# Decoder block in fp32 on one core: bias rows of the attention from ScalarE's queue, and other places for the sums of down's weights

## The chip, the cores and the metric

The kernel runs on one core of one Trainium2 chip. The metric is the device time of one execution in microseconds, the median of several; lower is better. The engines are named as in the profile: PE is TensorE, DVE is VectorE, ACT is ScalarE, POOL is GpSimd, SP is SyncE. Every engine works through its own program in order, and they wait for one another by semaphores.

## The reference

One residual block on 512 tokens of width 1024, one layer, everything in float32:

```python
h = rms_norm(x, norm1_g[l]) * (1 + scale1) + shift1
z = h @ w_in[l]
q, k, v, p, g_attn, g_pool = jnp.split(z, split_at, axis=-1)
...
attn = moba_attention(q, k, heads(v), rel_bias)
...
merged = (jax.nn.sigmoid(g_attn) * (attn @ w_branch_attn[l])
          + jax.nn.sigmoid(g_pool) * (pool @ w_branch_pool[l]))
x = x + gate1 * (merged @ w_out[l])
h2 = rms_norm(x, norm2_g[l]) * (1 + scale2) + shift2
u = causal_dwconv(h2 @ w_up[l], conv_w[l], conv_b[l])
u_g, u_v = jnp.split(u, 2, axis=-1)
x = x + gate2 * ((jax.nn.silu(u_g) * u_v) @ w_down[l])
```

The attention has 8 heads of 64 channels and a T5 bias on the logits that depends on the head and on the distance of query and key; with 512 tokens it is plain causal attention. shift, scale and gate (six groups of 1024) are `silu(c) @ ada_w + ada_b`. `w_up` is 1024 x 5632, `w_down` 2816 x 1024.

## The kernel before

Each fp32 matmul is done as three: both operands are split into a high part (`hi`, rounded to the matmul's type by ACT, L113) and a low part (`lo`, the remainder, subtracted by DVE, L123 or L219, in up also L1042), and hi·hi, lo·hi and hi·lo are summed (L132 to L134). So each block of weights needs a load by SP, ACT for hi and DVE for lo before PE can use all of it. The programs of PE, DVE and ACT stand in the order in which the code issues them; POOL and SP mostly issue DMAs, also in order. Buffers come from a pool of 72 tiles of 128x512 (`slot`), five raw weight tiles and 8 PSUM banks.

The stages follow one another: projections of p, q, k and v; the attention, a loop over heads h = 0 to 7; the branch loop, j = 0 to 7, in which the two branches are multiplied by their weights (`br`) and merged; the out stage over four token tiles t; the up stage, j = 0 to 21, each j a pair of a gate block and a value block, from j = 4 on every second one in a form with fewer matmuls; and down, in which products of sums of blocks are used.

**Bias rows.** `fd` in DRAM holds one row of bias per head. `logits(h)` first fetches that row shifted by one element for each partition into a slot, `trev` (L576, a DMA issued by POOL), then PE computes S (L587), DVE adds the bias and takes the minimum (L596), and ACT takes the exponential (L600); `softmax` scales by the reciprocal of the sum (L609 DVE, L610 ACT). In the loop over heads, `logits(h + 1)` and `softmax(h + 1)` are issued at the head of iteration h, after `flip(h)`, which transposes the probabilities of head h (PT). Behind them stand matmuls of the gates, the transposes and norms of Q and K for later heads (`stacks`), the product with v (`values(h)`, L637, which needs PT_l from DVE, L219), and two columns of the adaLN product (`ada_col`, L206 on DVE).

**Sums of down's weights.** Down needs sums of four blocks of `w_down`. They are formed once ahead, in eleven channel tiles kk = 0 to 10. `t_get(kk)` issues four loads of 256 KB on SP (L748); `t_do(kk)` forms four sums on DVE (L753 to L756, in place) and writes them to DRAM (`tsum`) with four DMAs issued by POOL (L758), from where down loads them. In the loop over heads iteration h issues `t_get(h)` for h < 5 and `t_do(h - 1)` for h = 1 to 5. The branch loop holds t_get 5 and 6 (j = 0, 1) and t_do 5 and 6 (j = 1, 2); the out stage t_get 7, 8, 9 and t_do 7, 8, 9 after `out_norm(t)`; up has t_get(10) ahead of j = 0 and t_do(10) at the end of j = 1. In the out stage POOL also issues the loads of x for the residual (L883, for t = 2 and 3 while the stage runs) and stores of the new x (`x2d`, L902); DVE adds to x (L892), forms the norm (xn, L899) and the low parts of the transposed h2 (`h2l`, L875).

**adaLN columns.** `ada_col(5, k)`, k = 0 to 7, runs in up at the j that `ADA_AT[k]` names.

Of the kernel before, what the change touches and what calls it, by code (L numbers as in the profile page):

```python
# [15 lines left out]
P = 128  # L16
S = 512
D = 1024
H = 8
# [36 lines left out]
def block_kernel(tc, x, cvec, ada, wtok, wch, pool_w, wbr, wout, wup, wdn, pack, table, out):  # L56
    nc = tc.nc
# [3 lines left out]
    with ctx:  # L61
# [11 lines left out]
        def slot(name, dt=F32, w=512):  # L73
            return sp.tile([P, w], dt, tag="s", name=name)
# [148 lines left out]
        fd = dpool.tile([H, NF], F32, name="fd")  # L223
# [278 lines left out]
        def fill(gen, us):  # L502
            while us > 0:
                c = next(gen, None)
                if c is None:
                    return
                us -= c
# [61 lines left out]
        ath, atl = [], []  # L569
        apair = {}  # L570

        def logits(h):

            trev = slot(f"trev_{h}")
            fsrc = fd[h : h + 1, :]
            nc.gpsimd.dma_start(  # L576
                trev, bass.AP(tensor=fsrc.tensor, offset=fsrc.offset, ap=[[1, P], [1, 512]]))
            ta = trev[:, :]
            pss = []
            for qt in (3, 2, 1, 0):  # L580
                n = max((qt + 1) * P, 256)
                if qt:
                    sb = bank(f"S_{h}_{qt}")
                    sps = sb
                else:
                    sps = sb[:, 256:]
                nc.tensor.matmul(sps[:, :n], Q[h][:, tslice(qt)], K2[h][:, :n], start=True, stop=False)  # L587
                nc.tensor.matmul(sps[:, :n], Q[h][:, tslice(qt)], K1[h][:, :n], start=False, stop=True)
                pss.append(sps)
            rows, sms = [], []  # L590
            for i, qt in enumerate((3, 2, 1, 0)):
                n = (qt + 1) * P
                L = slot(f"L_{h}_{qt}")
                mn = mini.tile([P, 1], F32, tag="mn", name=f"mn_{h}_{qt}")
                rev = bass.AP(tensor=ta.tensor, offset=ta.offset + n - 1, ap=[list(ta.ap[0]), [-1, n]])
                nc.vector.tensor_tensor_reduce(  # L596
                    out=L[:, :n], in0=pss[i][:, :n], in1=rev, op0=ALU.add, op1=ALU.min, scale=1.0,
                    scalar=3e38, accum_out=mn)
                sm = mini.tile([P, 1], F32, tag="sm", name=f"sm_{h}_{qt}")
                nc.scalar.activation(L[:, :n], L[:, :n], AF.Exp, scale=-1.0, bias=mn, accum_out=sm)  # L600
                rows.append(L)
                sms.append(sm)
            return rows, sms

        def softmax(h, rows, sms):
# [115 lines left out]
        fill(vgen, 1)  # L721
        stacks(0, True)
        fill(vgen, 2)
        stacks(1, True)
        stacks(0, False)
        fill(vgen, 5.5)
# [35 lines left out]
        def t_get(kk):  # L762
            tb[kk] = t_load(kk)

        def t_do(kk):
            t_forms(kk, tb.pop(kk))
# [10 lines left out]
        for h in range(H):  # L777
            pt = flip(h, rows)
            if h + 1 < H:
                rows = softmax(h + 1, *logits(h + 1))  # L780
            fill(gg, 3)
            if h % 2 == 0 and h < 6:
                stacks(h // 2 + 1, False)
            elif h in (1, 3):
                stacks((h + 3) // 2, True)
            values(h, *pt)
            ada_col(2, h)
            if h < 5:
                t_get(h)
            if 1 <= h < 6:  # L790
                t_do(h - 1)
            if h == 5:
                pooling(3)
            if h == 6:
                pool_proj(3)

            fill(gg, 3 if h < 5 else (share - 3) / 2)
            if h < 5:
                ada_col(3, h)
            fill(gg, (share - 3) / 2)  # L800
# [17 lines left out]
        for j in range(8):  # L818
            bw = unit(f"br{j}")
            ga, gp = gates[j], gates[8 + j]  # L820
            nc.scalar.activation(gp, gp, AF.Sigmoid)
            nc.scalar.activation(ga, ga, AF.Sigmoid)
            bps = bank(f"B_{j}")
            for k in range(4):
                mm3(bps, bw[0][:, tslice(4 + k)], bw[1][:, tslice(4 + k)], plh[k], pll[k], k == 0, k == 3)
            aps = bank(f"A_{j}")
            for k in range(4):
                mm3(aps, bw[0][:, tslice(k)], bw[1][:, tslice(k)], ath[k], atl[k], k == 0, k == 3)
            raw = load_unit(wout[j], f"wo{j}")
            for s in range(2):  # L830
                wo.append(split_act(raw[:, s * 512 : s * 512 + 512], f"wo{j}_{s}", eng=nc.gpsimd))
            nc.vector.tensor_mul(gp, gp, bps)
            nc.vector.tensor_mul(ga, ga, aps)
            if j < 2:
                t_get(5 + j)
            if 1 <= j <= 3:
                ada_col(3, 4 + j)
            nc.vector.tensor_add(gp, gp, ga)
            a, b = split_act(gp, f"mg_{j}")
            mgh.append(a)  # L840
            mgl.append(b)
            if 1 <= j < 3:
                t_do(4 + j)
            if j == 6:
                g1 = row_of(2, "g1")

# [57 lines left out]
        for t in range(TT):  # L904
            for f in range(2):
                if (t, f) == (0, 0):
                    for t_ in range(2):
                        for f_ in range(2):
                            out_mm(t_, f_, 0, KT - 2)
                if (t, f) != (3, 0):  # L910
                    out_mm(t, f, KT - 2 if t < 2 else 0, KT)
                    out_post(t, f, ops[t, f])
                if late:
                    ada_col(4, late.pop(0))
                    if not late:
                        nc.vector.scalar_tensor_tensor(acol[:, 32:40], acol[:, 32:40], 1.0, pk[:, C_N2 : C_N2 + 8],
                                                       op0=ALU.add, op1=ALU.mult)
            out_norm(t)
            if t < 3:
                t_get(7 + t)  # L920
            if t:
                t_do(6 + t)
            if t == 2:
                out_mm(3, 0, 0, KT)
                out_post(3, 0, ops[3, 0])
                flip_h2(1)
# [200 lines left out]
            keep(ug[:, R], X)  # L1127
            return ug, uv

        ADA_AT = [4, 6, 8, 10, 19, 20, 21, 21]  # L1130
        first = []
        for i in range(4):
            ahead(f"up{i}", min(2, 2 * PLAIN - 1 - i))
            first.append((ready.pop(f"up{i}"), bank(f"u_{i}")))
            up_mm(first[i][1], first[i][0], 0, 256)
            if i == 1:
                flip_h2(3)
                t_get(10)
        for w, ps in first:
            up_mm(ps, w, 256, 512)  # L1140
        pend, summed = [], []
# [15 lines left out]
        for j in range(NP):  # L1157
# [23 lines left out]
                up_mm(u[1], upw.pop((j, 1)), 0, S)  # L1181
                behind(1)
            pend.append((j, *u))
            if j == 1:
                t_do(10)
            for k in range(8):
                if ADA_AT[k] == j:
                    ada_col(5, k)
# [172 lines left out]
```

## Time and profile before

| | us |
|---|---|
| median of 3 runs | 721.94 (721.52 to 724.63) |
| the profiled execution | 726.77 |
| its span in the trace | 724.9 |
| TensorE busy in it | 676.9 |
| projections, up to the attention loop | about 0 to 115 |
| attention loop | about 115 to 264 |
| branch loop | about 265 to 318 |
| out stage | about 318 to 364 |
| up | about 364 to 614 |
| down | about 614 to 725 |

The stages overlap at their ends. The page gives two strips over 40 equal slices of the span, 18.1 us each: the share in which PE is busy, and the clock that PE was granted, in tenths:

```profile
PE   8999999988898599799979799999999999999997
PEclk9999999989989899899999999999999999999999
```

The first seven to eight slices are the projections. From there to the slice at 400 us the digits go up and down; from then on they stay at 9 up to the last.

### The profile page before, as it was taken

What the parts mean: (1) busy time and instruction counts of PE and PEld (TensorE: products, weight loads), DVE (VectorE), ACT (ScalarE), POOL (GpSimd) and SP (SyncE); (2) the same over time, 40 slices, a digit from 0 to 9 for tenths busy, and PEclk for the clock granted to TensorE, in tenths of its full rate; (3) what the DMA queues carried; (4) which work ended last, traced back from release to release, by engine and by line L of the source; (5) the groups of instructions that cost most, each with busy time, mean ns of one, the idle gap of its engine ahead of it and who ended that gap; (6) DMA issues with size and microseconds to landing.
All of it is one profiled execution on the core that took longest, in us unless ns stands there. A gap on an engine that the chain in (4) does not pass through costs nothing.

```text
span 724.9 us, 9576 instructions
## 1 busy us (share of the span) xinstructions
PE 676.9 (93%) x3403; PEld 571.7 (79%) x3403; DVE 560.1 (77%) x922; ACT 381.5 (53%) x663; POOL 93.5 (13%) x125
## 2 busy tenths in 40 slices
PE   8999999988898599799979799999999999999997
PEld 6778788866676487588869599888999988788885
DVE  7887865676656767887685989899897797978874
ACT  7455457745562554460353565565555553767440
POOL 3003310011100105570430100000000000001000
PEclk9999999989989899899999999999999999999999
DMA  9984243565555538969854234434232344577751
GB/s 353 306 273 145 91 131 112 206 212 178 196 175 170 160 114 217 363 217 334 322 191 159 94 111 134 135 109 140 94 117 90 114 146 160 182 242 248 269 190 58
DMA packets 41317, 131.51 MB, mean 181 GB/s; under 512 B 5315, under 2 KB 5484, under 8 KB 41270
## 3 DMA queue, kind: packets, MB, share of 16 engines
q1 hardware_dynamic: 34694, 109.77, 44.9%
q0 software_dynamic: 6576, 21.14, 8.8%
q8 instruction: 26, 0.43, 0.3%
q14 instruction: 21, 0.17, 0.1%
HBM read 115.13 MB, written 15.76 MB: 181 GB/s over the span
## 4 chain that ended last, share of the span: by engine, by line
PE 63%; DVE 12%; DMA 9%; issue 7%; ACT 6%; POOL 2%; SPq 0%; DVEq 0%; POOLq 0%; ACTq 0%
PE u L134 6%; PE u L132 6%; PE u L133 6%; DMA raw_p<-in_wtok 2%; PE X L139 2%; PE X L140 2%; PE X L138 2%; DVE raw_ada L206 2%; PE uX L140 2%; PE uX L139 2%; PE uX L138 2%; DMA trev<-fd 2%; DMA b<-in_wdn 2%; PE gate_ps L132 2%; PE gate_ps L133 2%
## 5 line engine op out<-in xcount | busy, mean ns | idle before, releaser
L134 PE MATMUL u<-h2h,lo_up 128*128 128x512 f32 (+1 forms) x256 | 94.5, 369 | 5.1 <-DVE lo_up L1042 3.0
L133 PE MATMUL u<-h2l,hi_up 128*128 128x512 f32 (+1 forms) x256 | 94.2, 368 | 2.8 <-DVE h2l L875 2.8
L132 PE MATMUL u<-h2h,hi_up 128*128 128x512 f32 (+1 forms) x256 | 94.5, 369 | 1.1 <-ACT hi_up L113 1.1
L206 DVE CUSTOM_DVE_ANT_0 raw_ada<-raw_ada,cbc,pk 128x1024 f32<-128x1024 f32 x48 | 61.2, 1286 | 3.7 <-DMA raw_ada<-in_ada 1.9
L134 PEld LDWEIGHTS u<-h2h,lo_up 128*128 128x128 f32 x256 | 49.3, 193 | 13.5 <-DVE lo_up L1042 3.4
L133 PEld LDWEIGHTS u<-h2l,hi_up 128*128 128x128 f32 x256 | 49.5, 194 | 10.3 <-DVE h2l L875 3.1
L132 PEld LDWEIGHTS u<-h2h,hi_up 128*128 128x128 f32 x256 | 49.5, 193 | 8.9 <-ACT hi_up L113 1.5
L132 PE MATMUL gate_ps<-h_h,hi_gate 128*128 128x512 f32 x128 | 53.4, 417 | 0.0
L133 PE MATMUL gate_ps<-h_l,hi_gate 128*128 128x512 f32 x128 | 53.1, 415 | 0.0
L134 PE MATMUL gate_ps<-h_h,lo_gate 128*128 128x512 f32 x128 | 52.6, 411 | 0.0
L758 POOL DMA_DIRECT2D tsum_t<-b x44 | 24.0, 546 | 145.7 <-DVE b L753 140.5
L600 ACT ACTIVATE L<-L,mn 128x512 f32<-128x512 f32 (+3 forms) x32 | 17.6, 552 | 46.4 <-DVE mn L596 46.4
L113 ACT ACTIVATE hi_up<-raw_up 128x1024 fp32r<-128x1024 f32 x28 | 29.3, 1049 | 7.2 <-PE u L133 7.2
L113 ACT ACTIVATE hi_t<-raw_t 128x1024 fp32r<-128x1024 f32 (+1 forms) x24 | 23.7, 987 | 17.5 <-PE Y L140 8.4
L123 DVE TENSOR_TENSOR lo_t<-raw_t,hi_t 128x1024 fp32r<-128x1024 f32 (+1 forms) x24 | 26.7, 1131 | 7.9 <-ACT hi_t L113 7.9
L1042 DVE TENSOR_TENSOR lo_up<-raw_up,hi_up 128x1024 fp32r<-128x1024 f32 x22 | 26.8, 1220 | 6.4 <-ACT hi_up L113 6.4
L807 POOL DMA_DIRECT2D g_d<-acol x2 | 1.8, 920 | 228.6 <-DVE acol L206 228.6
L134 PEld LDWEIGHTS gate_ps<-h_h,lo_gate 128*128 128x128 f32 x128 | 26.0, 203 | 5.9
L132 PEld LDWEIGHTS gate_ps<-h_h,hi_gate 128*128 128x128 f32 x128 | 26.2, 205 | 5.3
L133 PEld LDWEIGHTS gate_ps<-h_l,hi_gate 128*128 128x128 f32 x128 | 26.1, 204 | 5.2
L219 POOL TENSOR_TENSOR wo_l<-raw_wo,wo_h 128x512 fp32r<-128x512 f32 x16 | 25.7, 1619 | 14.6 <-ACT wo_h L218 14.4
L132 PE MATMUL o<-wo_h,mg_h 128*128 128x512 f32 x64 | 25.0, 391 | 0.0
(358 smaller groups left out, 1996.7 us busy)
## 6 DMA issues: line engine op xcount, KB each, us to landing
raw_ada<-in_ada SPq DMA_DIRECT2D x48, 512.0 KB, 5.0
raw_up<-in_wup SPq DMA_DIRECT2D x44, 512.0 KB, 3.3
b<-in_wdn SPq DMA_DIRECT2D x44, 256.0 KB, 7.2
tsum_t<-b POOLq DMA_DIRECT2D x44, 256.0 KB, 3.3
raw_t<-tsum_t SPq DMA_DIRECT2D x20, 512.0 KB, 5.2
raw_gate<-in_wch SPq DMA_DIRECT2D x16, 512.0 KB, 3.4
raw_b<-in_wdn SPq DMA_DIRECT2D x15, 512.0 KB, 3.3
raw_br<-in_wbr SPq DMA_DIRECT2D x8, 512.0 KB, 6.3
```

The costliest lines, as they stand in the source:

```text
L113: nc.scalar.activation(hi, raw, AF.Copy)
L123: nc.vector.tensor_sub(lo, raw, hi.bitcast(F32))
L132: nc.tensor.matmul(ps, sh, mh, start=start, stop=False)
L133: nc.tensor.matmul(ps, sh, ml, start=False, stop=False)
L134: nc.tensor.matmul(ps, sl, mh, start=False, stop=stop)
L138: nc.tensor.matmul(ps, sh, mh, start=start, stop=False, skip_group_check=True)
L139: nc.tensor.matmul(ps, sh, ml, start=False, stop=False, skip_group_check=True)
L140: nc.tensor.matmul(ps, sl, mh, start=False, stop=stop, skip_group_check=True)
L206: nc.vector.tensor_tensor_reduce(out=raw, in0=raw, in1=cbc, op0=ALU.mult, op1=ALU.add, scale=1.0, scalar=col(C_AB + i), accum_out=acol[:, ...
L219: (eng or nc.vector).tensor_sub(lo[:, :w], src, hi[:, :w].bitcast(F32))
L758: nc.gpsimd.dma_start(tsum[n, i][:, u * 512 : u * 512 + 512], b[nm])
L1042: nc.vector.tensor_sub(lo, raw, hi.bitcast(F32))
```

## The change

```diff
--- before.py
+++ after.py
@@ -569,13 +569,18 @@
         ath, atl = [], []
         apair = {}
 
+        trevs = {}
+
+        def trev_get(h):
+
+            trevs[h] = slot(f"trev_{h}")
+            fsrc = fd[h : h + 1, :]
+            nc.scalar.dma_start(
+                trevs[h], bass.AP(tensor=fsrc.tensor, offset=fsrc.offset, ap=[[1, P], [1, 512]]))
+
         def logits(h):
 
-            trev = slot(f"trev_{h}")
-            fsrc = fd[h : h + 1, :]
-            nc.gpsimd.dma_start(
-                trev, bass.AP(tensor=fsrc.tensor, offset=fsrc.offset, ap=[[1, P], [1, 512]]))
-            ta = trev[:, :]
+            ta = trevs.pop(h)[:, :]
             pss = []
             for qt in (3, 2, 1, 0):
                 n = max((qt + 1) * P, 256)
@@ -600,6 +605,8 @@
                 nc.scalar.activation(L[:, :n], L[:, :n], AF.Exp, scale=-1.0, bias=mn, accum_out=sm)
                 rows.append(L)
                 sms.append(sm)
+            if h + 1 < H:
+                trev_get(h + 1)
             return rows, sms
 
         def softmax(h, rows, sms):
@@ -721,6 +728,7 @@
         fill(vgen, 1)
         stacks(0, True)
         fill(vgen, 2)
+        trev_get(0)
         stacks(1, True)
         stacks(0, False)
         fill(vgen, 5.5)
@@ -785,9 +793,8 @@
                 stacks((h + 3) // 2, True)
             values(h, *pt)
             ada_col(2, h)
-            if h < 5:
-                t_get(h)
-            if 1 <= h < 6:
+            t_get(h)
+            if h:
                 t_do(h - 1)
             if h == 5:
                 pooling(3)
@@ -831,16 +838,14 @@
                 wo.append(split_act(raw[:, s * 512 : s * 512 + 512], f"wo{j}_{s}", eng=nc.gpsimd))
             nc.vector.tensor_mul(gp, gp, bps)
             nc.vector.tensor_mul(ga, ga, aps)
-            if j < 2:
-                t_get(5 + j)
             if 1 <= j <= 3:
                 ada_col(3, 4 + j)
             nc.vector.tensor_add(gp, gp, ga)
             a, b = split_act(gp, f"mg_{j}")
             mgh.append(a)
             mgl.append(b)
-            if 1 <= j < 3:
-                t_do(4 + j)
+            if j == 1:
+                t_do(7)
             if j == 6:
                 g1 = row_of(2, "g1")
 
@@ -916,10 +921,6 @@
                         nc.vector.scalar_tensor_tensor(acol[:, 32:40], acol[:, 32:40], 1.0, pk[:, C_N2 : C_N2 + 8],
                                                        op0=ALU.add, op1=ALU.mult)
             out_norm(t)
-            if t < 3:
-                t_get(7 + t)
-            if t:
-                t_do(6 + t)
             if t == 2:
                 out_mm(3, 0, 0, KT)
                 out_post(3, 0, ops[3, 0])
@@ -1127,7 +1128,8 @@
             keep(ug[:, R], X)
             return ug, uv
 
-        ADA_AT = [4, 6, 8, 10, 19, 20, 21, 21]
+        ADA_AT = [4, 6, 8, 10, 12, 14, 16, 18]
+        T_AT = [2, 20, 21]
         first = []
         for i in range(4):
             ahead(f"up{i}", min(2, 2 * PLAIN - 1 - i))
@@ -1135,7 +1137,6 @@
             up_mm(first[i][1], first[i][0], 0, 256)
             if i == 1:
                 flip_h2(3)
-                t_get(10)
         for w, ps in first:
             up_mm(ps, w, 256, 512)
         pend, summed = [], []
@@ -1181,8 +1182,10 @@
                 up_mm(u[1], upw.pop((j, 1)), 0, S)
                 behind(1)
             pend.append((j, *u))
-            if j == 1:
-                t_do(10)
+            if j + 1 in T_AT:
+                t_get(8 + T_AT.index(j + 1))
+            if j in T_AT:
+                t_do(8 + T_AT.index(j))
             for k in range(8):
                 if ADA_AT[k] == j:
                     ada_col(5, k)
```

Three things move. First, the fetch of the bias row is taken out of `logits` and put on ACT's queue, one head ahead: `trev_get(0)` stands in the stage of v, `trev_get(h + 1)` at the end of `logits(h)`, after the four exponentials. Second, the channel tiles of down's sums are placed anew: the loop over heads gets t_get 0 to 7 and t_do 0 to 6, the branch loop keeps t_do(7) at j = 1, the out stage has none, and up has t_get 8, 9, 10 at the end of j = 1, 19, 20 and t_do 8, 9, 10 at the end of j = 2, 20, 21. Third, the columns `ada_col(5, k)` of k = 4 to 7 stand at j = 12, 14, 16, 18 instead of 19, 20, 21, 21. PE's program keeps its order throughout. In the rows below, lines from L576 on are later in the changed code by some five to eight (L758 becomes L766, L610 L617).

POOL's program in the loop over heads, before (tsum: a write of a sum, b_0 and b_1 the channel tiles 0 and 1; trev: the fetch of a bias row):

```order
L758 DMA tsum_t_0_80<-b_0_1320 128x512
L758 DMA tsum_t_0_92<-b_0_1322 128x512
L758 DMA tsum_t_0_86<-b_0_1324 128x512
L758 DMA tsum_t_0_98<-b_0_1326 128x512
L576 DMA trev_1592<-fd 128x512
L758 DMA tsum_t_0_80<-b_1_1497 128x512
L758 DMA tsum_t_0_92<-b_1_1499 128x512
L758 DMA tsum_t_0_86<-b_1_1501 128x512
L758 DMA tsum_t_0_98<-b_1_1503 128x512
L576 DMA trev_1776<-fd 128x512
```

and with the change:

```order
L766 DMA tsum_t_0_80<-b_0_1322 128x512
L766 DMA tsum_t_0_92<-b_0_1324 128x512
L766 DMA tsum_t_0_86<-b_0_1326 128x512
L766 DMA tsum_t_0_98<-b_0_1328 128x512
L766 DMA tsum_t_0_80<-b_1_1499 128x512
L766 DMA tsum_t_0_92<-b_1_1501 128x512
L766 DMA tsum_t_0_86<-b_1_1503 128x512
L766 DMA tsum_t_0_98<-b_1_1505 128x512
```

Each fetch of trev stood behind four writes of sums; now the writes of one tile follow those of the one before, and no fetch is left on POOL.

ACT's program at the head of iteration 1, with the change; without its third row it is also that of before:

```order
L605 ACTIVATE L_1_1254,sm_1_1257<-L_1_1254,mn_1_1255 128x256
L605 ACTIVATE L_0_1259,sm_0_1262<-L_0_1259,mn_0_1260 128x128
L578 DMA trev_1264<-fd 128x512
L617 ACTIVATE L_3_1244<-L_3_1244,ri_3_1266 128x512
L617 ACTIVATE L_2_1249<-L_2_1249,ri_2_1269 128x384
L617 ACTIVATE L_1_1254<-L_1_1254,ri_1_1272 128x256
L617 ACTIVATE L_0_1259<-L_0_1259,ri_0_1275 128x128
```

The fetch for the next head stands between the last exponential and the first scaling of this head.

POOL's program in the out stage, before (x: load of the residual, x2d: store, rs_y: a step of the norm):

```order
L883 DMA x_2_0_3205<-in_x 128x512
L758 DMA tsum_t_3_83<-b_7_3146 128x512
L758 DMA tsum_t_3_95<-b_7_3148 128x512
L758 DMA tsum_t_3_89<-b_7_3150 128x512
L883 DMA x_2_1_3235<-in_x 128x512
L758 DMA tsum_t_3_101<-b_7_3152 128x512
L902 DMA x2d_0_3276<-x_2_0_3205 128x512
L902 DMA x2d_1_3280<-x_2_1_3235 128x512
L197 TENSOR_TENSOR rs_y_3272<-ms_y_3270,mhalf 128x1
L883 DMA x_3_0_3298<-in_x 128x512
L758 DMA tsum_t_4_84<-b_8_3189 128x512
L758 DMA tsum_t_4_96<-b_8_3191 128x512
```

and with the change:

```order
L888 DMA x_2_0_3197<-in_x 128x512
L888 DMA x_2_1_3227<-in_x 128x512
L907 DMA x2d_0_3268<-x_2_0_3197 128x512
L907 DMA x2d_1_3272<-x_2_1_3227 128x512
L197 TENSOR_TENSOR rs_y_3264<-ms_y_3262,mhalf 128x1
L888 DMA x_3_0_3274<-in_x 128x512
L907 DMA x2d_0_3393<-x_3_0_3274 128x512
L888 DMA x_3_1_3352<-in_x 128x512
L907 DMA x2d_1_3397<-x_3_1_3352 128x512
L197 TENSOR_TENSOR rs_y_3389<-ms_y_3387,mhalf 128x1
```

The writes of the sums of b_7 and b_8 stood around the loads of x; with the change there are none among them.

## The prediction

> **What bounds the kernel now.** I begin with the page: busy shares, and who owns the chain of work that ended last.
>
> ```profile
> span 724.9 us, 9576 instructions
> PE 676.9 (93%) x3403; PEld 571.7 (79%) x3403; DVE 560.1 (77%) x922; ACT 381.5 (53%) x663; POOL 93.5 (13%) x125
> PE 63%; DVE 12%; DMA 9%; issue 7%; ACT 6%; POOL 2%; SPq 0%; DVEq 0%; POOLq 0%; ACTq 0%
> ```
>
> TensorE is idle for only 48 us (724.9 − 676.9), so a change that removes no matmul can win that much and, beside it, matmul time spent at a lowered clock. The table by windows shows where (window, its length, busy time of PE, PEld, DVE, ACT, POOL; granted clock, DMA share, GB/s):
>
> ```profile
> 145.00:165.00 20.00, 16.57 (x74) 13.80 (x73) 13.32 (x28) 9.64 (x22) 2.72 (x5) 0.83 0.63 220
> 280.00:305.00 25.00, 19.10 (x71) 14.64 (x70) 20.02 (x25) 10.24 (x17) 11.91 (x13) 0.87 0.97 354
> 340.00:380.00 40.00, 35.05 (x194) 30.70 (x193) 29.81 (x61) 16.41 (x37) 15.02 (x27) 0.96 0.74 257
> 380.00:415.00 35.00, 30.95 (x190) 27.48 (x189) 26.11 (x40) 17.10 (x26) 2.17 (x4) 0.95 0.40 135
> 415.00:640.00 225.00, 223.40 (x1301) 198.17 (x1300) 201.36 (x300) 128.54 (x212) 2.01 (x3) 1.00 0.40 130
> ```
>
> Attention, branch loop, out stage and the start of up have holes and a lowered clock; the rest of up has neither (223.40 of 225 us), so nothing can be won there, only lost. The view of waits names what ends the holes (total us, times, longest):
>
> ```profile
> PE O L637 <- DVE PT_l L219: 13.4, 4, 3.6
> DVE L L596 <- DMA trev<-fd: 12.6, 4, 3.2
> PE S L587 <- ACT gate L499: 8.5, 2, 7.8
> PE B L134 <- DVE lo_br L123: 5.1, 2, 3.7
> ```
>
> The second row is VectorE's own wait; apart from the third (ACT's gate, which no part of the change touches), TensorE waits for VectorE, whose program is in order; the waits in out and up, further down, are of the same kind. Whatever holds VectorE ahead of these lines counts.
>
> **Bias rows, attention.** The timeline of one head and the chain of waits at the same place:
>
> ```profile
> 150.25 0.55 POOL L758 DMA_DIRECT2D tsum_t<-b  x1 [25.88 <-DVE b L753]
> 152.43 0.54 POOL L758 DMA_DIRECT2D tsum_t<-b  x1 [0.18 <-issue]
> 152.96 0.55 POOL L576 DMA_DIRECT2D trev<-fd  x1
> 153.30 0.33 SPq L81 DMA_DIRECT2D raw_ada<-in_ada  x1
> 152.96 7.18 DMA trev<-fd
> 155.53 1.61 DVE L219 TENSOR_TENSOR PT_l<-PT,PT_h 128x512 fp32r<-128x512 f32 x3
> 156.27 0.80 PE L637 MATMUL O<-PT_h,v 128*128 128x512 f32 x1 [3.43 <-DVE PT_l L219]
> 160.28 0.69 DVE L596 CUSTOM_DVE_ANT_0 L<-S,trev 128x512 f32<-128x512 f32 x1 [3.13 <-DMA trev<-fd]
> 177.52 1.62 DVE L219 TENSOR_TENSOR PT_l<-PT,PT_h 128x512 fp32r<-128x512 f32 x3
> ```
>
> GpSimd sits 25.88 us at the first tsum write, because that needs VectorE's add; the fetch of trev stands behind the four writes, starts at 152.96, takes 7.18 us, and VectorE waits 3.13 us for it. This happens four times, 12.6 us. One head then lasts 21.99 us from PT_l to PT_l (177.52 − 155.53). Of these TensorE idles 3.43 us, and in the window above the clock of 0.83 over 20 us is a loss of 3.4 us: its own work at full clock is some 15.2 us. So VectorE's row of work sets the period, and 18.9 us without the stall is still above 15.2: each microsecond of stall that goes is a microsecond of time, and the clock has nothing to add here, since a head at half clock (15.2 + 3.4 = 18.6) still fits.
>
> In the change the fetch is issued from ACT after the exponentials of the head before, about one period ahead, against 7.18 us of transfer: it is late by nothing with some 11 us to spare. Next to be late are the scalings and the gate's lo parts, the same row of VectorE work as now. The price: an issue on ACT, between the exponentials and the scalings that VectorE waits for. No row shows a DMA issue on ACT; the nearest are 0.33 us (SP) and 0.55 (GpSimd), and it can't be below nothing, as it only adds an instruction. I take 0.33, five heads: 1.7 us (0 to 2.8). **Attention: −12.6 + 1.7 = −10.9 us** (−9.8 to −12.6).
>
> The Trainium skill ("Trainium Kernel Development and Optimization", Key Constraints) says that DMAs from SP, ACT and POOL run on the same 16 engines and that issuing from several only saves issue time. By that the change would gain next to nothing here. The rows disagree: what is saved is not the 0.55 us of issue but the standing behind a write that waits for VectorE.
>
> **More sums in attention.** Heads 6 and 7 get t_do too, four adds each on VectorE:
>
> ```profile
> L753 DVE TENSOR_TENSOR b<-b,b 128x512 f32<-128x512 f32 x11 | 7.5, 686 | 2.4 <-DMA b<-in_wdn 2.4
> 259.06 1.23 DVE L123 TENSOR_TENSOR lo_br<-raw_br,hi_br 128x1024 fp32r<-128x1024 f32 x1 [1.63 <-ACT hi_br L113]
> 260.59 1.62 DVE L219 TENSOR_TENSOR PT_l<-PT,PT_h 128x512 fp32r<-128x512 f32 x3 [0.31 <-ACT PT_h L218]
> ```
>
> A group is four such adds, 2.8 us (the three others are of the same size). At head 6 VectorE idles 1.63 + 0.31 us, which covers all but 0.9 us of them. The loads, four issues on SP for each of heads 5 to 7, go out where the DMA engines are about 63% busy (the window from 145), and the tsum writes now have no fetch behind them on GpSimd. I take 0 for both heads; the bounds are 0 and +5.6, all eight adds on the path, and a gain is excluded, since work is added.
>
> **Branch loop.** The chain of waits, then the timeline:
>
> ```profile
> 285.53 8.30 DMA raw_br<-in_wbr
> 294.31 0.69 DVE L753 TENSOR_TENSOR b<-b,b 128x512 f32<-128x512 f32 x1
> 297.10 2.28 DVE L123 TENSOR_TENSOR lo_br<-raw_br,hi_br 128x1024 fp32r<-128x1024 f32 x1
> 299.43 0.79 PE L134 MATMUL B<-pl_h,lo_br 128*128 128x512 f32 x1 [3.65 <-DVE lo_br L123]
> 303.64 0.43 PE B L134
> 306.43 0.23 PE A L133
> ```
>
> Two groups of loads of b (b_5, b_6) share DMA engines that are 97% busy, raw_br takes 8.30 us behind them, and then the adds of b_6 (294.31 to 297.10, 2.8 us) stand ahead of lo_br. After the change one group (b_7) is loaded there instead of two, on SP ahead of this raw_br and no longer right before it, and no adds stand at j = 2; those at j = 1 stay. The adds alone give 2.8, the transfer the rest: the hole of 3.65 shrinks to about 0.45 (−3.2; bounds 0 and −3.65). Behind it matmuls take 0.43 us, still at 303.64, and 0.23 at 306.43: about six us at half clock, some 3.1 us lost, which go with the hole. **−6.3** (0 to −6.8).
>
> **Out stage.** Here x is fetched by GpSimd between the tsum writes, and the adds sit in VectorE's row:
>
> ```profile
> 352.12 0.54 POOL L883 DMA_DIRECT2D x<-in_x  x1
> 358.93 0.69 DVE L892 TENSOR_TENSOR x<-x,ot 128x512 f32<-128x512 f32 x1 [3.54 <-DMA x<-in_x]
> 366.69 0.39 PE L133 MATMUL u<-h2l,hi_up 128*128 128x256 f32 x1 [2.77 <-DVE h2l L875]
> 376.97 2.35 DVE L123 TENSOR_TENSOR lo_up<-raw_up,hi_up 128x1024 fp32r<-128x1024 f32 x2
> 378.24 0.39 PE L134 MATMUL u<-h2h,lo_up 128*128 128x256 f32 x1 [2.18 <-DVE lo_up L123]
> ```
>
> The adds of b_7 to b_9 stand here, three groups of 2.8 us, the last of them right ahead of the lo_up at 376.97; the x fetches stand behind tsum writes on GpSimd, and VectorE waits up to 3.54 us for them. With no sums there VectorE has 8.4 us less to do ahead of h2l and lo_up, and x comes sooner. Both holes (2.77 + 2.18) should go, and the clock of 0.96 over 40 us, another 1.6 us: 6.55 at most. I take **−6.0** (−3 to −6.6).
>
> **Start of up.**
>
> ```profile
> 406.45 1.04 ACT L113 ACTIVATE hi_up<-raw_up 128x1024 fp32r<-128x1024 f32 x1
> 407.18 0.69 DVE L753 TENSOR_TENSOR b<-b,b 128x512 f32<-128x512 f32 x1
> 409.96 1.22 DVE L1042 TENSOR_TENSOR lo_up<-raw_up,hi_up 128x1024 fp32r<-128x1024 f32 x1
> 411.23 0.72 PE L134 MATMUL u<-h2h,lo_up 128*128 128x512 f32 x1 [2.96 <-DVE lo_up L1042]
> ```
>
> Without the adds lo_up starts when hi_up ends (407.49) and not at 409.96: 2.5 of the 2.96 go, and with them the clock of 0.95 over 35 us (1.75): −4.2. But the adds of b_8 now come a step later, at j = 2, where VectorE may have just as little air. No row can show that; the bounds are 0 and the 4.2 that the adds cost now, and I give back the half, 2.1, between two ends that are equally near: **−2.1** (0 to −4.2).
>
> The Trainium skill ("TensorE: Matmul & The Clock Gate", "Why this matters for your kernels") warns of TensorE gaps over about 3 us. By that, the holes of 2.77 and 2.96 would not cost clock, and the sum would be 1.6 + 1.75 = 3.4 us smaller. The windows show 0.96 and 0.95 around them: the trace is stricter.
>
> **Rest of up.** The adaLN columns at 12 to 18 instead of 19 to 21, and two groups of adds at j = 20 and 21: in 415 to 640 VectorE is busy 201.36 of 225 us, 23.6 us of air for 5.6 us moved in and four columns moved within. TensorE's own work is the cover. I take 0: a gain is excluded by the 223.40 of 225, and with the cover gone the eight adds would cost 5.6 (bounds 0 and +5.6).
>
> **Sum**, against the profiled execution of 726.77 us: −10.9 − 6.3 − 6.0 − 2.1 = −25.3 us, 3.5%, so 701.5. The profiled execution lies 0.7% above the median of the runs, 721.94; carried over in proportion that is **696.8 us**. All terms at their best ends give −30.2 us and 692 us; with a third of the sum lost to the worse ends it is 705 us, and I take these two for the forecast's own range.
>
> **The rivals.**
> 1. *Only the bias rows pay.* The sums' adds merely stand elsewhere: in heads 6 and 7 and at j = 2 they delay as much as they did in the out stage. For it: VectorE is 77% busy and in order. Against it: VectorE's idle time at head 6, and 23.6 us of it in up. −10.9 us, 711.1 us.
> 2. *The adds of heads 6 and 7 lie on the path*: +5.6 less the 1.9 of air, with 3.4 of half clock behind them as in the window from 145: +7.1, sum −18.2, 703.9 us.
> 3. *The fetch stays late*, since it is the shared DMA engines that make it take 7.18 us; this is the case of the skill's rule on shared engines. The other terms remain, and the issues on ACT are paid: −14.4 + 1.7 = −12.7, 709.3 us. Against it: 11 us to spare.
> 4. *ACT blocks.* It is in order; a fetch of trev that has to wait for its buffer or its queue until a load of b has landed holds scalings, K and Q behind it, and through them VectorE and TensorE:
>
> ```profile
> b<-in_wdn SPq DMA_DIRECT2D x44, 256.0 KB, 7.2
> ```
>
> At 7.2 us for each of five heads that is +36 − 12.6 (the stall) − 14.4 = +9.0 us: slower, 730.9 us. From (12.6 + 14.4) / 5 = 5.4 us of wait a head on it wins over all gains. Against it: the load of b that it could wait for is issued in the head before, a period of some 20 us earlier, and should have landed.
> 5. *The change doesn't act*: another operand is late at the same places by as much (the hole of 7.8 us for ACT's gate stays anyway), and the sums come out even: 722 us.
>
> **How the numbers follow.** Chances: forecast 0.47, rival 1 0.20, rival 2 0.15, rival 3 0.06, rival 4 0.05, rival 5 0.07. The time is the forecast's. The range runs from 690, which is every term at its best end and 2 us for the spread of runs, to 711.5, which takes in rivals 1 to 3 and leaves out about 0.12 and what lies beyond. Within 0.5% is about what a measurement of this kernel can't tell from no change; faster by more: 0.47 + 0.20 + 0.15 + 0.06 = 0.88, same 0.07, slower 0.05.
>
> **What would show it.** In the profile of the changed kernel the wait of L's bias step for trev is gone and the heads 1 to 4 last some 19 us, with ACT showing no wait ahead of its scalings (rival 4: a wait of several us there; rival 3: trev still named). The hole ahead of B's lo_br falls under 1 us and the clock in the branch loop is 1.0; no wait for h2l and lo_up above 1 us in out; after the start of up TensorE stays within 1 us of full in each pair of steps. It fails if waits for PT_l and lo_br grow in heads 6 and 7, or if new waits for lo_upV come up at j = 2 to 4.

## The result, and the profile after

| | before | after |
|---|---|---|
| median (us) | 723.21 | 702.75 |
| ratio, 95% interval | | 0.9719 (0.9686 to 0.9752) |
| the profiled execution (us) | 726.77 | 704.26 |
| its span (us) | 724.9 | 702.0 |

The change makes the kernel 2.8% faster; the forecast of 696.8 us was 3.5%, and the measured time lies in the range. A second measurement of the same kernel, made beside the last experiments, gave 0.967 (0.9656 to 0.9684). One of the four runs of e1_pool_lead below took 819.66 us at a granted clock of 0.753; its ratio leaves that run out.

The page of the profile after, the same two rows as before:

```profile
PE 667.8 (95%) x3403; PEld 566.2 (81%) x3403; DVE 562.2 (80%) x922; ACT 380.7 (54%) x663; POOL 88.0 (13%) x117
PE 66%; DVE 17%; ACT 9%; issue 5%; DMA 2%; SPq 0%; ACTq 0%; DVEq 0%
```

DMA fell from 9% of the chain to 2%, and VectorE rose from 12% to 17%: what the transfers held is now held by VectorE's own row of work. The view of waits after (total us, times, longest):

```profile
PE O L644 <- DVE PT_l L219: 10.9, 4, 3.5
PE S L592 <- ACT gate L499: 6.2, 1, 6.2
PE B L134 <- DVE lo_br L123: 4.7, 2, 4.3
```

VectorE's wait for trev is gone from this view, and so are TensorE's waits for h2l and for the lo_up of the out stage (L123). The wait for lo_br has hardly shrunk (5.1 before). The timeline of one head after, to be held against the one of before:

```profile
155.15 1.61 DVE L219 TENSOR_TENSOR PT_l<-PT,PT_h 128x512 fp32r<-128x512 f32 x3
155.89 0.50 PE L644 MATMUL O<-PT_h,v 128*128 128x512 f32 x1 [3.42 <-DVE PT_l L219]
156.68 0.68 DVE L601 CUSTOM_DVE_ANT_0 L<-S,trev 128x512 f32<-128x512 f32 x1
158.17 0.60 ACT L605 ACTIVATE L<-L,mn 128x384 f32<-128x384 f32 x1
158.50 0.34 ACTq L578 DMA_DIRECT2D trev<-fd  x1
173.95 1.61 DVE L219 TENSOR_TENSOR PT_l<-PT,PT_h 128x512 fp32r<-128x512 f32 x3
174.69 0.50 PE L644 MATMUL O<-PT_h,v 128*128 128x512 f32 x1 [1.89 <-DVE PT_l L219]
```

L's bias step follows PT_l with no wait, and a head lasts 18.8 us (173.95 − 155.15) instead of 21.99. TensorE still waits for PT_l: VectorE's row remains the bound here.

TensorE's program is the same in all kernels of this study, so the start of one matmul can be compared between two traces. The sum of the differences at such matmuls (the start after, less the start before) makes a ledger of where the time went. Its five stations are the matmuls that start at 249, 320, 400, 420 and 440 us in the trace of before: behind the attention, behind the branch loop, in the first pairs of up, and behind the pair j = 4. The column for out also holds the first matmuls of up. From 440 us to the end the difference is nil in all but one kernel. Before's profiled execution took 726.77 us, 3.6 more than the median of its group, so the totals are somewhat larger than what the medians moved by.

| kernel (us against before's profile) | to 249 | branch | out | start of up | j = 4 | total |
|---|---|---|---|---|---|---|
| forecast | −10.9 | −6.3 | −6.0 | −2.1 (with j = 4) | | −25.3 |
| changed | −12.7 | −2.7 | −7.0 | −4.1 | +3.6 | −22.9 |
| changed, second profile (r1_changed) | −13.9 | −4.1 | −7.0 | −2.5 | +0.6 | −26.9 |
| e1_pool_lead | −12.6 | −4.1 | −7.0 | −2.5 | +0.6 | −25.6 |
| e2_act_nolead | −12.9 | −1.8 | −7.0 | −2.5 | +0.6 | −23.5 |
| e3_bias_only | −12.3 | −2.2 | −0.5 | −0.3 | 0.0 | −15.3 |
| e4_sums_only | −1.7 | −4.0 | −7.0 | −4.1 | +3.6 | −13.2 |
| e5_tdo7_j5 | −12.2 | −4.2 | −3.3 | −4.1 | +3.6 | −20.2 |
| e6_tdo8_j19 | −13.5 | −3.5 | −7.0 | −4.1 | 0.0 | −28.2 |
| e7_both | −12.3 | −4.8 | −4.0 | −4.1 | 0.0 | −25.1 |
| e8_ada_back | −14.0 | −4.1 | −7.0 | −4.1 | +3.6 | −23.7 (+1.8 in down) |
| r2_tdo8_j19 | −12.2 | −4.1 | −7.0 | −2.5 | 0.0 | −25.8 |
| e9_no_wol | −13.0 | −3.6 | −7.0 | −4.1 | +3.7 | −24.1 |
| e10_pool_first | −16.8 | −2.7 | −7.0 | −4.1 | 0.0 | −30.7 |

The out column takes one value for every kernel that has no sums in out and doesn't hold VectorE up ahead of it. The first two columns scatter by 1 to 2 us between executions; what an experiment says is read from the columns and from its ratio together.

### The profile page after: what moved, and what is told of

Read it like the earlier page. It is cut to its first block, busy times and chain, and to the rows that moved or that the text cites. A ratio compares the mean times of both kernels' runs of the same rounds, so it can differ in the third digit from the quotient of the medians.

```text
span 702.0 us, 9585 instructions
## 1 busy us (share of the span) xinstructions
PE 667.8 (95%) x3403; PEld 566.2 (81%) x3403; DVE 562.2 (80%) x922; ACT 380.7 (54%) x663; POOL 88.0 (13%) x117
## 4 chain that ended last, share of the span: by engine, by line
PE 66%; DVE 17%; ACT 9%; issue 5%; DMA 2%; SPq 0%; ACTq 0%; DVEq 0%
PE u L133 6%; PE u L132 6%; PE u L134 6%; DVE raw_ada L206 3%; PE X L139 2%; PE X L140 2%; PE X L138 2%; PE uX L138 2%; PE uX L140 2%; PE uX L139 2%; PE o L134 2%; PE o L133 2%; PE o L132 2%; DMA raw_p<-in_wtok 2%; ACT L L605 2%
## 5 line engine op out<-in xcount | busy, mean ns | idle before, releaser
L134 PE MATMUL u<-h2h,lo_up 128*128 128x512 f32 (+1 forms) x256 | 92.9, 363 | 0.5 <-DVE lo_up L1043 0.5
L133 PE MATMUL gate_ps<-h_l,hi_gate 128*128 128x512 f32 x128 | 51.6, 403 | 0.0
L766 POOL DMA_DIRECT2D tsum_t<-b x44 | 24.0, 546 | 205.2 <-DVE b L761 200.1
L113 ACT ACTIVATE hi_t<-raw_t 128x1024 fp32r<-128x1024 f32 (+1 forms) x24 | 23.7, 988 | 17.5 <-PE Y L140 8.4
L123 DVE TENSOR_TENSOR lo_t<-raw_t,hi_t 128x1024 fp32r<-128x1024 f32 (+1 forms) x24 | 26.6, 1131 | 8.0 <-ACT hi_t L113 7.9
L134 PEld LDWEIGHTS gate_ps<-h_h,lo_gate 128*128 128x128 f32 x128 | 25.1, 196 | 5.6
L133 PEld LDWEIGHTS gate_ps<-h_l,hi_gate 128*128 128x128 f32 x128 | 25.3, 198 | 4.9
L113 ACT ACTIVATE hi_b<-raw_b 128x1024 fp32r<-128x1024 f32 (+1 forms) x18 | 17.7, 984 | 13.6 <-PE X L140 8.1
```

The lines of the kernel that those rows point to most:

```text
L113: nc.scalar.activation(hi, raw, AF.Copy)
L123: nc.vector.tensor_sub(lo, raw, hi.bitcast(F32))
L133: nc.tensor.matmul(ps, sh, ml, start=False, stop=False)
L134: nc.tensor.matmul(ps, sl, mh, start=False, stop=stop)
```

## The experiments

Ratios are to the kernel before, run on the same chip, with their 95% intervals.

**Lead or queue.** The change moves the fetch of the bias row to another queue and issues it one head earlier. Two kernels do one without the other, with the sums as changed.

e1_pool_lead: GpSimd's queue, one head ahead.

```diff
-            nc.scalar.dma_start(
+            nc.gpsimd.dma_start(
                 trevs[h], bass.AP(tensor=fsrc.tensor, offset=fsrc.offset, ap=[[1, P], [1, 512]]))
```

> The changed kernel with the bias row fetched on GpSimd's queue again, but still one head ahead; sums as changed. If the lead is what helps (each fetch then stands behind sums that were added a whole head earlier, and has a period of 18.8 us for a transfer of 5 to 7 us), no wait for trev comes back and the time is that of the changed kernel, 0.972 of before (about 702.8 us). If the queue is what helps, the wait of about 3 us a head comes back: +12, about 715 us, 0.989.

Measured: 702.31 us, 0.9679 (0.9659 to 0.9699). GpSimd's timeline in it:

```profile
187.39 0.54 POOL L766 DMA_DIRECT2D tsum_t<-b  x1 [13.95 <-DVE b L761]
189.56 0.54 POOL L766 DMA_DIRECT2D tsum_t<-b  x1 [0.18 <-issue]
190.09 0.55 POOL L578 DMA_DIRECT2D trev<-fd  x1
```

The fetch still stands behind four writes that waited 13.95 us for VectorE, and takes 7.3 us from there to its landing, but it is that of the next head (first used at 212.96), and nobody waits for it. The lead alone is enough.

e2_act_nolead: ACT's queue, issued at the start of the same head's logits.

```diff
         def logits(h):
 
+            trev_get(h)
             ta = trevs.pop(h)[:, :]
...
-            if h + 1 < H:
-                trev_get(h + 1)
             return rows, sms
...
-        trev_get(0)
         stacks(1, True)
```

> The changed kernel with the fetch on ACT's queue, but issued at the start of the same head's logits, as before; sums as changed. If leaving the queue of the tsum writes is enough, the fetch goes out right behind PT_h, some 1.3 us sooner than it did on GpSimd, and lands in 5.3 us instead of 7.2: the wait falls from 3.1 us a head to 0.6 us or less, time 702 to 705 us, 0.972 to 0.976. If the lead is needed, 2 us a head or more remain: above 711 us, 0.983.

Measured: 702.94 us, 0.9696 (0.9667 to 0.9726), and no wait for trev in the trace. So leaving the queue of the writes is enough as well. But that moved the time of issue too, and by more than the 1.3 us that were expected (timeline of e2, a fetch and its first use):

```profile
148.38 0.33 ACTq L578 DMA_DIRECT2D trev<-fd  x1
157.64 0.68 DVE L602 CUSTOM_DVE_ANT_0 L<-S,trev 128x512 f32<-128x512 f32 x1
```

The fetch goes out 9.3 us ahead of its use, and 2.5 us ahead of the split PT_h (150.89) that stands before it in ACT's program. In the four heads that waited in the kernel before, it went out 4.1 to 4.2 us ahead of the moment at which VectorE was ready (7.2 to 7.4 us, less the wait); in e2 it is 5.6 to 9.4 us in the same heads. The fetch is also shorter; the view of the tile in this kernel:

```profile
L578 ACTq DMA_DIRECT2D trev<-fd x8: 326/326/344, 103.6 to 230.3; - x8
DMA to landing us min/median/max: 3.0/3.1/5.1
```

The trace holds the landing of only three of the eight fetches, so these are the three values. Behind the four writes of sums it took 6.8 to 7.3 us in the four heads that waited before, and 6.6 to 7.4 in the last four of e1. How much of the cure in e2 is the earlier issue and how much the shorter transfer, no run separates.

**The parts alone.** e3_bias_only is the kernel before with the first part only; e4_sums_only is the changed kernel with the fetch as it was (GpSimd's queue, same head).

The first, against before:

```diff
+        def trev_get(h):
+            trevs[h] = slot(f"trev_{h}")
...
+            nc.scalar.dma_start(
+                trevs[h], bass.AP(tensor=fsrc.tensor, offset=fsrc.offset, ap=[[1, P], [1, 512]]))
...
+            if h + 1 < H:
+                trev_get(h + 1)
             return rows, sms
```

> The kernel before with the bias rows alone changed (ACT's queue, one head ahead); sums and adaLN columns as before. By the ledger of the two traces (attention 12.7 us shorter) about 710.5 us, 0.9825. If the holes of branch and out grow because TensorE arrives earlier while VectorE's row there is as long as it was, part of it is taken back: 713 to 718 us, 0.987 to 0.993.

The second, against the changed kernel, has the edits of e2_act_nolead and this one:

```diff
-            nc.scalar.dma_start(
+            nc.gpsimd.dma_start(
```

> The kernel before with the sums and the adaLN columns moved as in the change, and the bias rows as before (GpSimd's queue, same head). If the two parts add up, the stalls of 12.6 us remain and what branch, out and up gave (10 us) is gained: about 713 us, 0.986. If the sums' move is worth something only with the bias rows (two more heads whose fetch stands behind tsum writes: up to 6 us more of stalls), 717 to 720 us, 0.992 to 0.996.

Measured: 712.55 us, 0.9837 (0.9809 to 0.9866), and 714.48 us, 0.9851 (0.9831 to 0.987). The product is 0.9690, between the two measurements of the whole change (0.9719 and 0.967): the parts add up, and rival 1 of the prediction, that only the bias rows pay, is out. In the ledger e3 has the attention's column and e4 has those of out and up; e4 keeps its wait for trev, as the view of waits has it:

```profile
DVE L L602 <- DMA trev<-fd: 11.0, 4, 3.0
```

Four times again, although two more heads have sums: those heads' time is not set by the fetch. e4 differs from e1 by the lead alone and from e2 by the queue alone, in the same group of measurements: each is worth some 12 us (714.48 against 702.31 and 702.94).

**The hole ahead of lo_br.** In the profile of the changed kernel the second largest hole of TensorE was new, ahead of lo_br at j = 4, where there were 1.46 us before. VectorE, GpSimd and PE in it, three pieces of the timeline:

```profile
272.62 0.68 DVE L761 TENSOR_TENSOR b<-b,b 128x512 f32<-128x512 f32 x1
274.79 1.93 DVE L764 TENSOR_TENSOR b<-b,b 128x512 f32<-128x512 f32 x1
276.64 2.40 DVE L123 TENSOR_TENSOR lo_br<-raw_br,hi_br 128x1024 fp32r<-128x1024 f32 x1
...
274.89 1.27 POOL L219 TENSOR_TENSOR wo_l<-raw_wo,wo_h 128x512 fp32r<-128x512 f32 x1
276.67 1.27 POOL L219 TENSOR_TENSOR wo_l<-raw_wo,wo_h 128x512 fp32r<-128x512 f32 x1
...
279.09 0.50 PE L134 MATMUL B<-pl_h,lo_br 128*128 128x512 f32 x1 [4.27 <-DVE lo_br L123]
```

Two things stand out: the adds of t_do(7) right ahead of lo_br, and operations of VectorE that take two to three times as long as elsewhere (0.69 and 1.22 us) beside an operation of GpSimd. One experiment for each.

e5_tdo7_j5:

```diff
-            if j == 1:
+            if j == 5:
                 t_do(7)
```

> The changed kernel with t_do(7) at j = 5 of the branch loop instead of j = 1. If the four adds ahead of lo_br make the new hole of 4.27 us there, it falls to 1.5 us or less and the half clock behind it goes: 3 to 4 us faster than the changed kernel, about 699 us, 0.967 of before. If VectorE's row in the branch loop is full anyway, the adds delay lo_br at j = 6 instead and nothing is won: 702.8 us, 0.972.

Measured: 705.67 us, 0.9721 (0.9699 to 0.9743): no gain. The hole ahead of lo_br at j = 4 shrinks to 0.53 us, but this came in its place (timeline of VectorE and PE, then a piece of the chain of waits):

```profile
300.25 0.68 DVE L761 TENSOR_TENSOR b<-b,b 128x512 f32<-128x512 f32 x1
302.41 3.77 DVE L764 TENSOR_TENSOR b<-b,b 128x512 f32<-128x512 f32 x1
...
349.48 0.39 PE L133 MATMUL u<-h2l,hi_up 128*128 128x256 f32 x1 [1.97 <-DVE h2l L880]
```

```profile
317.26 7.76 DMA raw_ada<-in_ada
```

The four adds held VectorE for 5.9 us (300.25 to 306.18), the last one, beside GpSimd, for 3.77 alone. VectorE's row came into the out stage later; as the chain has it, the load of an adaLN column starts late there, x follows, and 43 us behind the adds TensorE waits at h2l. The out column of the ledger falls from −7.0 to −3.3. Expected was a gain or nothing; that it would be given back in out was not foreseen.

e9_no_wol leaves out GpSimd's part of the branch loop, the low parts of w_out, so its output is another one.

```diff
-                wo.append(split_act(raw[:, s * 512 : s * 512 + 512], f"wo{j}_{s}", eng=nc.gpsimd))
+                wo_h = slot(f"wo{j}_{s}_h", F32R)
+                nc.scalar.activation(wo_h, raw[:, s * 512 : s * 512 + 512], AF.Copy)
+                wo.append((wo_h, wo_h))
```

> The changed kernel without GpSimd's splits of w_out in the branch loop: the low parts aren't computed, the high part stands in for them, so the output differs; 16 operations of GpSimd and 16 tiles fall away. If VectorE's operations there are long (lo_br 2.40 instead of 1.22 us, the gate products 1.7 to 2.3 instead of 0.68) because GpSimd works beside them, all of them have their short durations, the hole ahead of lo_br is under 1.5 us, and the time is 2 to 5 us below the changed kernel. If they are long for another reason (load of the DMA engines, 0.98 there), durations and hole stay, and so does the time within 1 us.

Measured: 703.97 us, 0.9683 (0.9655 to 0.9711), no less than the changed kernel beside it. The expectation holds for the durations and fails for the time. Timeline of VectorE and of ACT in it:

```profile
261.41 0.69 DVE L845 TENSOR_TENSOR gate<-gate,gate 128x512 f32<-128x512 f32 x1
271.53 0.69 DVE L764 TENSOR_TENSOR b<-b,b 128x512 f32<-128x512 f32 x1
274.93 1.23 DVE L123 TENSOR_TENSOR lo_br<-raw_br,hi_br 128x1024 fp32r<-128x1024 f32 x1 [2.71 <-ACT hi_br L113]
...
273.84 1.06 ACT L113 ACTIVATE hi_br<-raw_br 128x1024 fp32r<-128x1024 f32 x1 [5.13 <-DMA raw_br<-in_wbr]
```

All eight sums of the two gated branches (gate<-gate,gate; the expectation calls them gate products) take 0.69 us now (0.98 to 2.32 in the changed kernel, but for one of 0.68, which ran beside no operation of GpSimd). So it is GpSimd's work beside them that stretches VectorE's. But the weights of the branch then come too late (5.13 us of wait, 1.54 at the same place in the second profile of the changed kernel): VectorE and the loads end almost together, and shortening one gives the other its turn. So the branch loop has two bounds, and the forecast had reckoned with one. How large the hole ahead of lo_br comes out differs from kernel to kernel where the programs up to there are alike: 4.27 in the first profile of the change, 1.31 in the second, 4.92 in e2, 2.93 in e1, 1.86 in e8 and r2, 0.73 in e6.

r1_changed is the changed kernel once more, in the same group as e9, r2 and e10.

> The changed kernel again, unaltered, beside the variants of this group. 0.968 to 0.972 of before; the hole ahead of lo_br in the branch loop, 4.27 us in its first profile and 1.9 to 4.9 in kernels that are alike up to there, comes out at another size again if it hangs on which operations of VectorE and GpSimd happen to overlap.

Measured: 702.05 us, 0.967 (0.9656 to 0.9684), with the hole at 1.31 us: another size again. At j = 6 it has two waits that before's profile doesn't have (timeline of PE):

```profile
288.51 0.50 PE L132 MATMUL B<-pl_h,hi_br 128*128 128x512 f32 x1 [0.79 <-ACT hi_br L113]
289.77 0.50 PE L134 MATMUL B<-pl_h,lo_br 128*128 128x512 f32 x1 [0.53 <-DVE lo_br L123]
```

**The sums in up.** e6_tdo8_j19, and r2_tdo8_j19, the same kernel measured beside r1:

```diff
-        T_AT = [2, 20, 21]
+        T_AT = [19, 20, 21]
```

> The changed kernel with t_get(8) and t_do(8) at the ends of j = 18 and 19 instead of 1 and 2. If the adds at j = 2 make the hole of 1.90 us ahead of hi_upR's matmuls at j = 4 and the half clock behind it, 2.7 us go: about 700 us, 0.968 of before. If three groups at j = 19 to 21 are one too many for VectorE, a new hole of about 2.8 us opens there and the time stays at 702.8 us, 0.972.

> The variant with t_do(8) at j = 19 again. 2.7 us (0.4%) faster than the changed kernel of this group if the adds at j = 2 are what costs; equal to it if the earlier gain came from the branch loop's scatter.

Measured: 698.6 us, 0.9633 (0.9607 to 0.9659), and 700.82 us, 0.9645 (0.9629 to 0.9662), 1.2 us under r1 in the same group. In the changed kernel's profile the adds at j = 2 put VectorE late for the matmuls of j = 4 (timeline):

```profile
390.88 0.68 DVE L761 TENSOR_TENSOR b<-b,b 128x512 f32<-128x512 f32 x1
394.26 1.22 DVE L1060 TENSOR_TENSOR lo_upG<-raw_up,hi_upG 128x1024 fp32r<-128x1024 f32 x1
...
401.83 0.39 PE L138 MATMUL uX<-hs_h,hi_upR 128*128 128x256 f32 x1 [1.90 <-ACT ka L1108]
```

In both profiles with t_do(8) at j = 19 the column j = 4 is 0.0; with it at j = 2 it is +3.6 or +0.6. Three groups at the end of up open no hole. In sign the reason is right; the size of 2.7 us holds for some executions only, and the median gained 1.2, where the runs of each kernel spread over 1.4 and 2.2 us.

e7_both joins e5 and e6:

> Both: t_do(7) at j = 5 of the branch loop, t_do(8) at j = 19 of up. If the holes are those of the two groups of adds, the gains add up: 6 to 7 us faster than the changed kernel, 696 to 697 us, 0.963 of before. If neither is, 702.8 us, 0.972.

Measured: 702.0 us, 0.9681 (0.9658 to 0.9704). The gains don't add up: the ledger shows e6's 0.0 at j = 4 and e5's loss in out (−4.0 instead of −7.0).

e8_ada_back puts the adaLN columns back:

```diff
-        ADA_AT = [4, 6, 8, 10, 12, 14, 16, 18]
+        ADA_AT = [4, 6, 8, 10, 19, 20, 21, 21]
```

> The changed kernel with the adaLN columns of up at 19, 20, 21, 21 again instead of 12, 14, 16, 18. If VectorE has air enough in either place, the time stays at 702.8 us, 0.972 of before. If t_do(9) and t_do(10) at j = 20 and 21 need the room that the columns left, four columns of 1.3 us more there open a hole of up to 5 us: 704 to 708 us, 0.974 to 0.980.

Measured: 703.09 us, 0.9682 (0.966 to 0.9705), the same as the changed kernel within the intervals. Its profile shows 1.8 us more at the start of down, where the hole ahead of lo_b is 1.77 instead of 1.60 us and half clock follows; whether the columns cause that, the times don't settle.

**A version that goes further.** The largest hole that is left stands in head 5, where S waits for ACT's gate. e10_pool_first starts from e6:

```diff
             t_get(h)
-            if h:
-                t_do(h - 1)
             if h == 5:
                 pooling(3)
+            if h:
+                t_do(h - 1)
```

> The variant with t_do(8) at j = 19, and in head 5 the pooling ahead of the four adds of t_do(4) on VectorE, not behind them. TensorE waits 6.2 us there for ACT's gate, which stands behind ACT's pool_h, which waits for VectorE's pooling. If the adds are part of that chain, the hole shrinks by 2.8 us and perhaps its half clock by 3.4: 2.8 to 6 us below the variant, 0.955 to 0.960 of before. If the adds then hold the gate's lo parts by as much, the hole moves to PT_l or the next lo_gate and the time stays.

Measured: 697.46 us, 0.9603 (0.9589 to 0.9617), 3.4 us under r2 and the fastest kernel here. The matmul behind the hole in r2, and then in e10:

```profile
230.62 0.58 PE L592 MATMUL S<-kz,Q 128*128 128x256 f32 x1 [6.18 <-ACT gate L499]
```

```profile
226.74 0.39 PE L592 MATMUL S<-kz,Q 128*128 128x256 f32 x1 [3.38 <-ACT gate L499]
```

The hole shrank by 2.80 us, the four adds' length: they had stood ahead of the pooling that ACT and, through it, TensorE were waiting for. In the ledger the attention gains 4.6 us and the branch loop gives 1.4 back: there TensorE now waits 1.83 us for hi_br at j = 4, and ACT 3.1 us for its weights, the second bound again.

## Why the prediction was right, point by point

- **Bias rows.** Right in mechanism, −12.7 to −13.9 us at the end of the attention against −10.9. Most of the difference is the price of ACT's issue, put at 1.7 and measured at nothing: e1, which issues no fetch on ACT, has −12.6 in the same column. In the changed kernel the row of 0.34 us at 158.50 lies beside an exponential that runs at the time (158.17 to 158.77), and the scalings start 0.39 us behind the last exponential's start as they did before (159.65 after 159.26; 163.27 after 162.88). Rivals 3 and 4 didn't come about; no wait of ACT or VectorE has the fetch as its cause. One reading in it was wrong: that no part of the change touches the hole for ACT's gate. It fell from 7.79 us to 6.16 in the first profile, 4.57 in the second and 4.56 in e3, and stayed at 7.47 in e4, which keeps the stall: that gate waits for VectorE's pooling (e10), which the stall had held too. By the Trainium skill's sentence on queues that share 16 engines ("Trainium Kernel Development and Optimization", Key Constraints), the move should have saved issue time only. e4 and e2, which differ in the queue alone, lie 11.5 us apart: what was saved is a place in line, and part of the transfer.
- **Adds in heads 6 and 7.** Put at 0. No new wait for PT_l shows in either head. The adds start at 242.31 and 256.44 us of the changed profile, behind the ledger's first station; from there to the matmul at 286.90 us of before, ahead of the hole at j = 4, the difference moves by 0.0 us in the first profile of the change, by 0.5 in the second, and by 0.0 in e3, which has no adds there. Rival 2 is out.
- **Branch loop.** This is the term that was mis-sized: −6.3 forecast, −2.7 and −4.1 measured. For j = 5 it was right: the hole of 3.65 us did go, and its half clock with it, which gave 6.1 us in the second profile (from 288.97 to 305.14 us of before). The step that failed is "those at j = 1 stay", put down at no cost. The hole behind those adds was 1.46 us before; in the first profile of the change, where they fall beside GpSimd's splits as in the rows above, it is 4.27, half clock follows, and 4.4 us are lost (to 291.83 us of before). In the second it is 1.31, but 1.5 us are given back at j = 6 by the waits of 0.79 and 0.53 us shown above. e9 and e10 show that the loads of the weights stand close behind as a second bound.
- **Out stage.** −6.0 forecast, −7.0 measured, 0.4 more than the "at most" of 6.55; both holes went and so did the clock loss. e3, which leaves the sums in out, keeps both holes.
- **Start of up.** −2.1 forecast, −0.5 and −2.0 measured (−4.1 + 3.6 and −2.5 + 0.6). To give back half of what the adds cost was a choice between two far ends; that it came close in the second profile is luck. e6 and r2 show that what is given back at j = 4 is due to t_do(8) at j = 2; the rest of the difference between the two profiles is a stretch of half clock (last section).
- **Rest of up.** 0 forecast, 0.0 in the ledger.
- **Sum.** −25.3 forecast, −22.9 between the profiles of the first measurement and −26.9 for the second execution's profile. That it comes so near is in part luck: in the first profile attention and out gave 2.8 us more than forecast, branch and up 5.2 less. The medians moved by 20.5 and by 24.3 us. Of the 5.9 us by which 696.8 missed 702.75, some 4.7 are gain that didn't come, and 1.3 come from before's median, 723.21 here and 721.94 in the forecast.
- **Signs.** The wait for trev went, a head lasts 18.8 us, and the waits for h2l and lo_up in out are gone. Two signs did not come out: the hole ahead of lo_br did not fall under 1 us (4.27 and 1.31), with the clock at half behind it in the first profile, and a wait of 1.90 us came up at j = 4 of up.

## What to carry to other kernels

A small fetch that shares an in-order queue with writes that wait for another engine inherits that wait, and its transfer was longer behind them (6.6 to 7.4 us, against 3.0 to 5.7 on ACT's queue); either a queue without such writes or one iteration of lead cures it, and both together bring nothing more. Work that can stand anywhere is best put where the engine idles, and not just off the stage that complains: a group of four adds cost nothing in the last heads and at the end of up, 0.6 or 3.6 us at j = 2, and 2.8 us ahead of a pooling that others waited for. Before a stage's gain is booked, ask for its second bound; here the branch loop's loads ended almost with VectorE's row.

## What the runs showed of the hardware that was not expected

**The clock is granted by windows, and half a window of idle time is enough.** In each of the fourteen profiles the stretches at half clock start on a grid of 3.41 us. I summed TensorE's idle time in each window of that grid between 110 and 620 us. Every window at full clock with 1.97 us or more of idle time (58%) was followed by one at half clock, and none with 1.54 us or less was; between them both occur. Leaving half clock took less idle time still: each window at half clock with 0.72 us or more of it was followed by another, each with 0.35 us or less by one at full clock. The holes needn't be one piece. In the second profile of the changed kernel, two short ones (timeline of PE, then the table by windows):

```profile
382.54 0.50 PE L132 MATMUL u<-h2h,hi_up 128*128 128x512 f32 x1 [1.03 <-ACT hi_up L113]
383.80 0.63 PE L134 MATMUL u<-h2h,lo_up 128*128 128x512 f32 x1 [0.53 <-DVE lo_up L1043]
```

```profile
380.00:384.00 4.00, 2.45 (x10) 1.43 (x9) 3.62 (x6) 3.30 (x6) 0.00 (x0) 1.00 0.00 0
384.00:387.40 3.40, 3.40 (x9) 2.62 (x9) 3.33 (x5) 2.44 (x4) 0.00 (x0) 0.50 0.51 154
```

Holes of 1.03 and 0.53 us fell into one window and cost a window at half clock. In the first profile the same two holes fell into two windows and cost none; that is the −4.1 and −2.5 of the start of up. What followed evened out: TensorE at half clock came later to j = 4, where the hole then was 0.31 instead of 1.90 us. So a part of the scatter between executions of one program is where the holes happen to fall on the grid.

**A DMA issued on ACT's queue cost ACT nothing** (0.33 us of the queue's time beside a running operation), while GpSimd's issues take 0.55 us of its own. It also went out ahead of operations that stand before it in ACT's program: at 158.50 us in the changed kernel, with the last two exponentials starting at 158.77 and 159.26, and in e2 2.5 us ahead of PT_h.

**GpSimd's elementwise work stretches some of VectorE's:** sums of the gated branches of 0.69 us alone took up to 2.3, an add of 0.69 up to 3.77, a lo part of 1.22 up to 2.40. All of these read two tiles of the pool. The products gate<-gate,B and gate<-gate,A, whose second operand stands in a PSUM bank, took 0.67 to 0.69 us in all fourteen profiles, although 195 of the 224 ran beside an elementwise operation of GpSimd.
